# Three issue orders in a hybrid retention and sparse-attention block: angle tables behind the squares' sum, first indexer scores and the latent's sum of squares behind projection matmuls

## The chip, the cores and the metric

The kernel runs on one core of a Trainium2 chip. The metric is the device time of one execution in microseconds (us), as the median of three runs. A core has five engines, each with its own instruction queue that is worked off in order: TensorE (PE), VectorE (DVE), ScalarE (ACT), GpSimd (POOL) and SyncE (SP, which here only issues DMAs).

## The reference

One layer over 1024 tokens of width 1024, one batch, fp32:

```python
h = rms_norm(x, norm_mix)
proj = h @ w_in        # one projection, split into the inputs of both head groups
a = retention(rotary(r_q), rotary(r_k), r_v)            # 8 heads of 64, chunks of 64
c_kv = rms_norm(d_c, kv_norm)                           # latent of width 128
b = sparse_attention(q_nope, q_pe, c_kv, k_pe, i_q, i_k, i_w, w_uk, w_uv)
# per token: score = sum_h i_w[h] * relu(i_q[h] . i_k * 32**-0.5), the 256 best keys,
# then softmax attention over these keys alone
y = concat(norm(a) * silu(r_g), b * silu(d_g)) @ w_out + x
y = y + sigmoid(rms_norm(y, norm_ple) @ w_ple_gate) * (p @ w_ple_proj)
out = rms_norm(y, norm_final)
```

## The kernel before

Tokens are taken in 8 tiles of 128. Matrix products are made to fp32 accuracy by splitting both operands into a high and a low part and adding three products (hi·hi, hi·lo, lo·hi); ACT writes the high part of a weight (`whi`, L222) and POOL the low part (`wlo`, L223). The work is written as a program of tiles, and a scheduler with a modelled timeline sets the order of the instructions on each engine from the data dependences, the buffers and priorities; the engines then work their queues off in order.

**Input stage.** x is loaded transposed in 8 pieces. `load_x` makes xhi on ACT (L257) and xlo on DVE (L258). `add_squares` squares each piece on ACT (L265) and adds it to `acc` on DVE (L266). PE runs the first projection as pieces come (L300 to L302), then sums `acc` over the partitions (L365), and DVE and POOL make the reciprocal root `rstd` of it (`rsqrt`, L314 to L323; POOL's power at L319). The angle tables cos and sin for the indexer (cosx, sinx) and for retention (cosr, sinr) are made by `angles` and `tables` (L330 to L343): DVE reduces the angles (L331, L335, L336, three passes of L338, L339), ACT takes the sines and squares (L340 to L342). `spread` (L349 to L355) turns rstd into a row over all partitions, `rstd_b`, and the tables are multiplied by it (L369).

**Projections.** `n_chunk` (L461 to L492) makes token-major projections: per chunk of 256 columns and per token tile 24 matmuls of 128x256 (L472 to L474; called N below), evacuated by ACT (nst, L475), finished on POOL (L485) and stored by SP (L490) or ACT (L492); chunks come in the order 2, 3, 0, 1 and then 4, 5. The first N need a PSUM bank that ACT frees by copying the first projection out (L360, `it`). `t_block` (L304 to L312) makes column-major blocks of 48 matmuls of 128x512 (called T): blocks 0 to 7 are retention's, block 8 the latent, blocks 9 to 11 the attention's queries.

**Indexer.** The indexer's queries and keys are rotated (L378 to L384), split (`il`, POOL L238), stored to DRAM (L392 to L415) and loaded again as `ks` (L431) and per token tile as `qs` (L436, L437). Score matmuls (L449) run by token tile in the order TI = 7, 6, 4, 2, 3, 5; ACT takes the relu (`rel`, L450), DVE adds the heads up (`sc`, L452 and L454).

**Search and choice.** For each row of tokens the threshold of the 256th score is searched on keys made by DVE (`key`, L600, L601): three tiles on DVE (counts L624, thresholds L633 to L650) and three on ACT (counts L640, L643, L645). The choice steps on DVE (L677 to L689) then write the mask `bias` for each tile.

**Latent.** Block 8 gives the latent; `cq` is its square (ACT L523), `pk` its sum over partitions on PE (L526).

**Rest.** `prep_v` (L722 to L731, ACT L730 and DVE L731 make the values' high and low parts `vd`) and `prep_k` (L733 to L745) prepare the attention; `retention_load` (SP L789) and `retention_split` (ACT L803, DVE L804: `qz`) prepare retention. Then attention, retention, output projection, gate and last norm run.

Of the kernel before, what the change touches and what calls it, by code (L numbers as in the profile page):

```python
# [15 lines left out]
OP = mybir.AluOpType  # L16
# [6 lines left out]
NT = 8  # L23
# [25 lines left out]
TI = [7, 6, 4, 2, 3, 5]  # L49
# [104 lines left out]
def _body(ctx, nc, tc, ap, dbg):  # L154
    V, A, G, T, Y = nc.vector, nc.scalar, nc.gpsimd, nc.tensor, nc.sync

    def f(t):
        return t.bitcast(F32)

    def pool(name, **kw):  # L160
        return tc.tile_pool(name=name, bufs=kw.pop("bufs", 1), reuse_waits="tile", **kw)

# [18 lines left out]
    ones1 = cpool.tile([128, 1], F32, name="ones1")  # L181
# [31 lines left out]
    xhi = [xpool.tile([128, S], FR, name=f"xhi{k}") for k in range(NT)]  # L213
    xlo = [xpool.tile([128, S], FR, name=f"xlo{k}") for k in range(NT)]
# [28 lines left out]
    acc = p1p.tile([128, S], F32, name="acc")  # L243
# [16 lines left out]
    def add_squares(k):  # L260
        raw = raws[k // 2][:, k % 2]
        if k == 0:
            A.activation(acc, raw, AF.Square)
        else:
            A.activation(raw, raw, AF.Square)  # L265
            V.tensor_tensor(out=acc, in0=acc, in1=raw, op=OP.add)  # L266

    w1 = []
    zero = p1p.tile([128, 512], BF, name="zero")
# [6 lines left out]
    for k in range(NT):  # L276
# [6 lines left out]
            Y.dma_start(posi, rows_to_all(ap["pos"], S))  # L283
        if k > 0:
            add_squares(k - 1)
    add_squares(NT - 1)
    Y.dma_start(same, ap["cst"][:, CF:CN])
    Y.dma_start(retn_b, rows_to_all(ap["ret_norm"], 512))

# [14 lines left out]
    def t_block(b, outs):  # L304
        ws = [load_w(ap["w_t"][b, kg], 128) for kg in range(2)]
        for h in range(2):
            sl = slice(512 * h, 512 * h + 512)
            for k in range(NT):
                wh, wl = (t[:, k % 4] for t in ws[k // 4])
                T.matmul(outs[h], wh, xhi[k][:, sl], start=k == 0, stop=False)  # L310
                T.matmul(outs[h], wh, xlo[k][:, sl], start=False, stop=False)  # L311
                T.matmul(outs[h], wl, xhi[k][:, sl], start=False, stop=k == 7)  # L312

    def rsqrt(out, ssum, n, w):  # L314
        a = tiny.tile([128, 16], F32, name="rs_a")[:, :w]
# [11 lines left out]
    cosx = wk("cosx")  # L327
    sinx = wk("sinx")

    def angles(col, cos_t):  # L330
        V.tensor_scalar(cos_t, posi, cst[:, CV + col:CV + col + 1], None, op0=OP.mult)  # L331

    def tables(cos_t, sin_t):
        ang, kk = cos_t, sin_t
        V.tensor_scalar(kk, ang, 1.0 / (2.0 * math.pi), MAGIC, op0=OP.mult, op1=OP.add)  # L335
        V.tensor_scalar(kk, kk, -MAGIC, None, op0=OP.add)  # L336
        for c in CODY:
            V.scalar_tensor_tensor(ang, kk, -c, ang, op0=OP.mult, op1=OP.add)  # L338
        V.tensor_scalar(ang, ang, PI_LO, -PI_LO, op0=OP.min, op1=OP.max)  # L339
        A.activation(sin_t, ang, AF.Sin)  # L340
        A.activation(cos_t, ang, AF.Sin, scale=0.5)
        A.activation(cos_t, cos_t, AF.Square)  # L342
        V.tensor_scalar(cos_t, cos_t, -2.0, 1.0, op0=OP.mult, op1=OP.add)  # L343

    angles(1, cosx)
    tables(cosx, sinx)
    angles(0, cosr)

    def spread(dst, col):  # L349
        for h in range(2):  # L350
# [81 lines left out]
    for i in TI:  # L432
        w = 128 * (i + 1)
        qs = ixp.tile([96, 8, 128], FR, name="qs", bufs=2)
        tsl = slice(128 * i, 128 * i + 128)
        Y.dma_start(f(qs)[0:64], d_iq[:, :, :, tsl].rearrange("n r h t -> (n r) h t"))  # L436
        Y.dma_start(f(qs)[64:96], d_iq[0, :, :, tsl])  # L437
        so = OFF[i] - OFF[2]
        dst = sc[:, so:so + w]
        for h in range(8):  # L440
            rel = wk("rel")
            if h % 4 > 1 if w <= 512 else h % 3 > 1:
                pbs = [(c0, min(w, c0 + 512), nb("ib")) for c0 in range(0, w, 512)]
            else:
                pbs = [(0, w, big())]
            for b0, b1, pb in pbs:
                for c0 in range(b0, b1, 512):
                    c1 = min(b1, c0 + 512)
                    T.matmul(pb[:, c0 - b0:c1 - b0], qs[:, h], ks[:, c0:c1], start=True, stop=True)  # L449
                A.activation(rel[:, b0:b1], pb[:, :b1 - b0], AF.Relu, scale=32.0 ** -0.5)  # L450
            if h == 0:
                V.tensor_scalar(dst, rel[:, :w], wi[:, i, 0:1], 0.0, op0=OP.mult, op1=OP.add)  # L452
            else:
                V.scalar_tensor_tensor(dst, rel[:, :w], wi[:, i, h:h + 1], dst, op0=OP.mult, op1=OP.add)  # L454
        V.memset(sc[0:64, so + w - 64:so + w], -3.0e38)
# [5 lines left out]
    def n_chunk(c, func, place=nb):  # L461
        ws = [load_w(ap["w_n"][c, kg], 256) for kg in range(4)]
        for tg in range(2):
            for a in range(4):
# [5 lines left out]
                for k in range(NT):  # L470
                    wh, wl = (t[:, k % 2] for t in ws[k // 2])
                    T.matmul(pb[:, a % 2], xhi[k][:, tsl], wh, start=k == 0, stop=False)  # L472
                    T.matmul(pb[:, a % 2], xhi[k][:, tsl], wl, start=False, stop=False)  # L473
                    T.matmul(pb[:, a % 2], xlo[k][:, tsl], wh, start=False, stop=k == 7)  # L474
                A.activation(st[:, a % 2], pb[:, a % 2], func, scale=rstd[:, j:j + 1])  # L475
                if a % 2 == 0:
                    continue
# [45 lines left out]
    A.activation(cq, cr, AF.Square)  # L523
    pk = nb("ib")
    for j in range(NT):
        T.matmul(pk[:, j:j + 1], cq[:, 128 * j:128 * j + 128], ones1, start=True, stop=True)  # L526
    rkv = cpool.tile([128, NT], F32, name="rkv")
    rsqrt(rkv, pk[:, :NT], 128, NT)

# [699 lines left out]
```

## Time and profile before

| | |
|---|---|
| median of 3 runs | 828.8 us (828.28 to 830.05) |
| profiled execution | 826.33 us |
| its span in the profile | 824.5 us |
| mean granted TensorE clock | 0.969 |
| PE busy | 763.3 us, 93% |
| DVE busy | 596.7 us, 72% |
| ACT busy | 477.3 us, 58% |
| POOL busy | 313.6 us, 38% |

The span runs from the first to the last instruction in the profile; the execution's own time is 1.8 us longer. The busy shares are means over stages with different limits, so a stage has to be read by itself.

### The profile page before, as it was taken

Reading aid. Unit: us, or ns where it says so; the run is one execution under the profiler, and the core shown is the slowest. Engines: PE = TensorE matmul, PEld = TensorE weight load, DVE = VectorE, ACT = ScalarE, POOL = GpSimd, SP = SyncE. Lnnn points to the kernel's source line nnn. Section 1 sums busy time; section 2 is a strip of 40 time slices with the busy share of each in tenths; the row PEclk is TensorE's granted clock in tenths of the full one; section 3 lists DMA queues with packets and bytes.
Section 4 is the critical chain, followed back from the end, with each engine's and each line's share of the span. In section 5 each row is a group of like instructions: output and inputs, shape, how many; then the busy total and the mean of one; then the engine's idle time right before and its main releaser. Section 6 shows DMA issues by size and latency. Waiting matters only on the chain.

```text
span 824.5 us, 12686 instructions
## 1 busy us (share of the span) xinstructions
PE 763.3 (93%) x4415; PEld 661.8 (80%) x4415; DVE 596.7 (72%) x1270; ACT 477.3 (58%) x1041; POOL 313.6 (38%) x237
## 2 busy tenths in 40 slices
PE   8979699979999979999889887999999999899995
PEld 5768699968888868998788776788878887688885
DVE  5948178999999999998768777556565655653655
ACT  7543267729995699971667565543464454334333
POOL 3725625452775544730037667520261101310110
PEclk9979899989999999999999998999999999999999
DMA  8312924221533122532647755773554446542511
GB/s 316 99 40 93 235 76 115 65 78 31 179 101 112 52 103 85 177 113 77 166 116 197 204 157 172 237 249 133 158 190 172 161 172 206 202 153 78 178 52 52
DMA packets 68159, 114.42 MB, mean 139 GB/s; under 512 B 6048, under 2 KB 37664, under 8 KB 68096
## 3 DMA queue, kind: packets, MB, share of 16 engines
q1 hardware_dynamic: 64480, 107.06, 41.9%
q10 hardware_dynamic: 3616, 6.55, 2.2%
q8 instruction: 35, 0.57, 0.3%
q14 instruction: 28, 0.23, 0.1%
HBM read 75.97 MB, written 37.62 MB: 138 GB/s over the span
## 4 chain that ended last, share of the span: by engine, by line
PE 50%; DVE 31%; ACT 5%; DMA 5%; issue 4%; POOL 2%; SPq 1%; POOLq 0%; ACTq 0%; DVEq 0%
DVE res L624 8%; PE lg L1146 6%; PE rb L1146 5%; PE rb L1076 4%; PE rb L1077 3%; PE rb L1078 3%; PE tp L937 3%; PE nb L472 2%; PE nb L473 2%; PE nb L474 2%; DMA qk<-d_f 2%; PE lg L915 1%; PE oo L973 1%; PE lg L914 1%; PE oo L972 1%
## 5 line engine op out<-in xcount | busy, mean ns | idle before, releaser
L640 ACT ACTIVATE ajunk<-key,cthr 128x1024 bf16<-128x1024 int16 (+5 forms) x96 | 95.7, 997 | 27.5 <-DVE key L601 15.0
L223 POOL TENSOR_TENSOR wlo<-wraw,whi 128x512 fp32r<-128x512 f32 (+1 forms) x58 | 88.0, 1533 | 53.6 <-ACT whi L222 53.5
L473 PE MATMUL nb<-wlo,xhi 128*128 128x256 f32 x256 | 74.5, 292 | 5.5 <-POOL wlo L223 5.5
L472 PE MATMUL nb<-whi,xhi 128*128 128x256 f32 x256 | 75.0, 295 | 2.2 <-ACT nst L475 1.5
L624 DVE TENSOR_SCALAR_CACHE_REDUCE res<-key,athr 128x384 f32<-128x384 int16 (+5 forms) x96 | 75.5, 786 | 1.8
L474 PE MATMUL nb<-whi,xlo 128*128 128x256 f32 x256 | 74.3, 291 | 0.0
L319 POOL TENSOR_TENSOR rs_y<-rs_a,mhalf 128x1 f32<-128x1 f32 (+1 forms) x26 | 27.1, 1046 | 122.8 <-DVE rs_a L318 120.3
L944 DVE TENSOR_TENSOR t<-tp,t 128x512 fp32r<-128x512 f32 (+1 forms) x72 | 45.7, 643 | 30.3 <-ACT t L943 29.9
L920 ACT ACTIVATE lm<-lm,mxv 128x128 f32<-128x128 f32 (+3 forms) x64 | 49.3, 772 | 21.4 <-DVE mxv L919 20.9
L943 ACT ACTIVATE t<-tp 128x512 fp32r<-128x512 f32 (+1 forms) x72 | 39.0, 556 | 37.8 <-PE oo L973 27.2
L310 PE MATMUL big<-xhi,whi 128*128 128x512 f32 x144 | 56.1, 392 | 0.4 <-DVE mb L384 0.4
L311 PE MATMUL big<-xlo,whi 128*128 128x512 f32 x144 | 56.2, 391 | 0.0
L473 PEld LDWEIGHTS nb<-wlo,xhi 128*128 128x128 f32 x256 | 51.1, 200 | 6.3 <-POOL wlo L223 5.7
L312 PE MATMUL big<-xhi,wlo 128*128 128x512 f32 x144 | 55.8, 390 | 0.0
L472 PEld LDWEIGHTS nb<-whi,xhi 128*128 128x128 f32 x256 | 50.9, 200 | 4.3 <-ACT nst L475 2.7
L454 DVE SCALAR_TENSOR_TENSOR sc<-rel,wi,sc 128x1024 f32<-128x1024 f32 (+5 forms) x42 | 47.3, 1129 | 7.5 <-ACT rel L450 4.9
L474 PEld LDWEIGHTS nb<-whi,xlo 128*128 128x128 f32 x256 | 51.0, 199 | 0.7
L937 PE MATMUL tp<-cst,lm 128*128 128x128 f32 x288 | 47.8, 282 | 2.9 <-DVE t L944 2.1
L916 DVE CUSTOM_DVE_ANT_0 lm<-lg,bias 128x512 f32<-128x512 f32 (+2 forms) x64 | 36.7, 585 | 13.6 <-PE tp L937 6.4
L937 PEld LDWEIGHTS tp<-cst,lm 128*128 128x128 f32 x288 | 35.2, 145 | 9.0 <-DVE t L944 3.8
L222 ACT ACTIVATE whi<-wraw 128x512 fp32r<-128x512 f32 (+1 forms) x58 | 34.9, 611 | 12.3 <-PE nb L474 3.0
L972 PE MATMUL oo<-t,vd 128*128 128x256 f32 (+1 forms) x144 | 38.6, 287 | 3.1 <-ACT t L943 2.6
(497 smaller groups left out, 2451.6 us busy)
## 6 DMA issues: line engine op xcount, KB each, us to landing
wraw<-in_w_t SPq DMA_DIRECT2D x26, 256.0 KB, 2.8
wraw<-in_w_n SPq DMA_DIRECT2D x24, 256.0 KB, 2.7
d_f<-o SPq DMA_DIRECT2D x8, 512.0 KB, 3.1
qk<-d_f SPq DMA_DIRECT2D x16, 256.0 KB, 3.5
ql<-d_qs SPq DMA_DIRECT2D x16, 256.0 KB, 5.2
qh<-d_qs SPq DMA_DIRECT2D x32, 128.0 KB, 4.8
twr<-in_w_out SPq DMA_DIRECT2D x8, 512.0 KB, 5.6
xt<-in_x SPq DMA_DIRECT2D x8, 512.0 KB, 4.1
```

The lines of the kernel that those rows point to most:

```text
L223: G.tensor_tensor(out=lo, in0=raw, in1=f(hi), op=OP.subtract)
L310: T.matmul(outs[h], wh, xhi[k][:, sl], start=k == 0, stop=False)
L311: T.matmul(outs[h], wh, xlo[k][:, sl], start=False, stop=False)
L312: T.matmul(outs[h], wl, xhi[k][:, sl], start=False, stop=k == 7)
L472: T.matmul(pb[:, a % 2], xhi[k][:, tsl], wh, start=k == 0, stop=False)
L473: T.matmul(pb[:, a % 2], xhi[k][:, tsl], wl, start=False, stop=False)
L474: T.matmul(pb[:, a % 2], xlo[k][:, tsl], wh, start=False, stop=k == 7)
L624: V.tensor_scalar(junk, src[:, KS[i]], thr[:, n:n + 1], 0.0, op0=op, op1=OP.add, accum_out=cnt[:, n:n + 1])
L640: A.activation(junk[:, :128 * (i + 1)], src[:, KS[i]], AF.Sign, bias=self.thr[:, n:n + 1], accum_out=cnt[:, n:n + 1])
L920: A.activation(lm[:, :w], lm[:, :w], AF.Exp, bias=mx, scale=0.125, accum_out=den[:, a, h:h + 1])
L937: T.transpose(tp[:, o:o + 128], pt[a][:, ks_], ident)
L1146: T.matmul(po[c.start // 512][:, c.start % 512:c.start % 512 + c.stop - c.start], a, b[:, c], start=k == 0 and m == 0, stop=k == n - 1 and ...
```

## The change

Three orders of issue are added; no operation is added, taken away or resized.

1. `angles` and `tables` are traced inside a block that puts every instruction they issue on DVE behind the last add of squares, `squares`, which `add_squares` now returns.
2. The score matmuls of the first two tiles in TI (7 and 6) get an ordering edge behind the last matmul that `n_chunk` issues for chunk 3, tile 2.
3. The eight matmuls of `pk` get an ordering edge behind the last matmul of the first half of block 9, the first query block.

All three are edges between instructions of one engine, so none adds a semaphore. The scheduler lays everything else out anew around them.

```diff
+    marks = {}
+    def behind(ins, mark):
+        marks.setdefault(mark, []).append(ins)
+    def mark(name, ins):
+        for x in marks.pop(name, []):
+            tc.add_manual_dep(x.ins, ins.ins.name,
+                              mybir.DependencyInfo(mybir.DependencyClass.NoSync, mybir.DependencyReason.DATA),
+                              reason="order of issue")
...
-            V.tensor_tensor(out=acc, in0=acc, in1=raw, op=OP.add)
+            return V.tensor_tensor(out=acc, in0=acc, in1=raw, op=OP.add)
...
-    add_squares(NT - 1)
+    squares = add_squares(NT - 1)
...
-                T.matmul(outs[h], wl, xhi[k][:, sl], start=False, stop=k == 7)
+                last = T.matmul(outs[h], wl, xhi[k][:, sl], start=False, stop=k == 7)
+            if h == 0:
+                mark(f"block {b}", last)
...
-    angles(1, cosx)
-    tables(cosx, sinx)
-    angles(0, cosr)
+    with tc.issue_after(squares.ins):
+        angles(1, cosx)
+        tables(cosx, sinx)
+        angles(0, cosr)
...
-                    T.matmul(pb[:, c0 - b0:c1 - b0], qs[:, h], ks[:, c0:c1], start=True, stop=True)
+                    m = T.matmul(pb[:, c0 - b0:c1 - b0], qs[:, h], ks[:, c0:c1], start=True, stop=True)
+                    if i in TI[:2]:
+                        behind(m, "chunk 3 tile 2")
...
-                    T.matmul(pb[:, a % 2], xlo[k][:, tsl], wh, start=False, stop=k == 7)
+                    last = T.matmul(pb[:, a % 2], xlo[k][:, tsl], wh, start=False, stop=k == 7)
+                mark(f"chunk {c} tile {j}", last)
...
-        T.matmul(pk[:, j:j + 1], cq[:, 128 * j:128 * j + 128], ones1, start=True, stop=True)
+        behind(T.matmul(pk[:, j:j + 1], cq[:, 128 * j:128 * j + 128], ones1, start=True, stop=True), "block 9")
```

**DVE, input stage.** acc is the sum of squares, xlo the low parts of x, cosx, sinx, cosr, sinr the tables on their way. Before:

```order
L338 SCALAR_TENSOR_TENSOR cosx<-sinx,cosx 128x1024
L258 SCALAR_TENSOR_TENSOR xlo_120<-xraw,vecs,xhi_112 128x1024
L258 SCALAR_TENSOR_TENSOR xlo_121<-xraw,vecs,xhi_113 128x1024
L338 SCALAR_TENSOR_TENSOR cosr<-sinr,cosr 128x1024
L266 TENSOR_TENSOR acc<-acc,xraw 128x1024
L338 SCALAR_TENSOR_TENSOR cosx<-sinx,cosx 128x1024
L338 SCALAR_TENSOR_TENSOR cosr<-sinr,cosr 128x1024
L266 TENSOR_TENSOR acc<-acc,xraw 128x1024
L338 SCALAR_TENSOR_TENSOR cosx<-sinx,cosx 128x1024
L338 SCALAR_TENSOR_TENSOR cosr<-sinr,cosr 128x1024
L266 TENSOR_TENSOR acc<-acc,xraw 128x1024
L339 TENSOR_SCALAR cosx<-cosx 128x1024
```

and of the change, where line 258 is 270, 266 is 278, 331 is 345, 335 is 349 and 336 is 350:

```order
L278 TENSOR_TENSOR acc<-acc,xraw 128x1024
L270 SCALAR_TENSOR_TENSOR xlo_119<-xraw,vecs,xhi_111 128x1024
L278 TENSOR_TENSOR acc<-acc,xraw 128x1024 x2
L270 SCALAR_TENSOR_TENSOR xlo_120<-xraw,vecs,xhi_112 128x1024
L270 SCALAR_TENSOR_TENSOR xlo_121<-xraw,vecs,xhi_113 128x1024
L278 TENSOR_TENSOR acc<-acc,xraw 128x1024 x2
L345 TENSOR_SCALAR cosx<-posi,cst 128x1024
L345 TENSOR_SCALAR cosr<-posi,cst 128x1024
L349 TENSOR_SCALAR sinx<-cosx 128x1024
L349 TENSOR_SCALAR sinr<-cosr 128x1024
L350 TENSOR_SCALAR sinx<-sinx 128x1024
L350 TENSOR_SCALAR sinr<-sinr 128x1024
```

Before, seven passes of the tables stand between these low parts and sums, and others ahead of them; now all low parts and sums come first, and the fourteen table passes follow in one stretch, ahead of `rs_a` of `rsqrt`.

**PE, where the first score matmuls stand.** nb <- whi, wlo, xlo are N matmuls, big and ib <- ks, qs the scores. Before:

```order
L474 MATMUL nb<-whi,xlo_120 128x256
L472 MATMUL nb<-whi,xhi_113 128x256
L473 MATMUL nb<-wlo,xhi_113 128x256
L474 MATMUL nb<-whi,xlo_121 128x256
L472 MATMUL nb<-whi,xhi_110 128x256
L449 MATMUL big<-ks,qs 128x512 x4
L449 MATMUL ib<-ks,qs 128x512 x2
L473 MATMUL nb<-wlo,xhi_110 128x256
L474 MATMUL nb<-whi,xlo_118 128x256
```

and of the change, where lines 472 to 474 are 489 to 491 and 449 is 464:

```order
L491 MATMUL nb<-whi,xlo_120 128x256
L489 MATMUL nb<-whi,xhi_113 128x256
L490 MATMUL nb<-wlo,xhi_113 128x256
L491 MATMUL nb<-whi,xlo_121 128x256
L464 MATMUL big<-ks,qs 128x512 x4
L464 MATMUL ib<-ks,qs 128x512 x2
L489 MATMUL nb<-whi,xhi_106 128x256
L490 MATMUL nb<-wlo,xhi_106 128x256
L491 MATMUL nb<-whi,xlo_114 128x256
```

Before, 205 N stand between the sum over partitions and the first score, the last of them in the middle of a tile; now 240 N, ten whole tiles, stand there. The transposes of `spread` stand behind 38 N instead of 48. To the last score of tile 2 there are 347 N from the first score, 355 before. The `pk` matmuls move by three matmuls: behind 36 of the 48 of block 9 instead of 33.

**DVE, choice steps.** qz is retention's split, vd the values, the other lines are the choice of one tile. Before:

```order
L686 SCALAR_TENSOR_TENSOR res<-junk 128x768
L687 SCALAR_TENSOR_TENSOR junk<-res,aneed,junk 128x768
L804 TENSOR_TENSOR qz_4551<-qk,qz_4550 64x4x128 x2
L688 SCALAR_TENSOR_TENSOR junk<-sc,akfin,junk 128x768
L689 TENSOR_SCALAR bias<-junk 128x768
L804 TENSOR_TENSOR qz_4556<-qk,qz_4555 64x4x128 x2
...
L687 SCALAR_TENSOR_TENSOR junk<-res,cneed,junk 128x640
L688 SCALAR_TENSOR_TENSOR junk<-sc,ckfin,junk 128x640
L689 TENSOR_SCALAR bias<-junk 128x640
L731 TENSOR_TENSOR vd_4365<-lg,vd_4365 128x8x64
L731 TENSOR_TENSOR vd_4366<-rb,vd_4366 128x8x64
L731 TENSOR_TENSOR vd_4367<-lg,vd_4367 128x8x64
```

and of the change, where line 687 is 705, 688 is 706, 804 is 822 and 731 is 749:

```order
L705 SCALAR_TENSOR_TENSOR junk<-res,aneed,junk 128x384
L822 TENSOR_TENSOR qz_4551<-qk,qz_4550 64x4x128
L706 SCALAR_TENSOR_TENSOR junk<-sc,akfin,junk 128x384
L822 TENSOR_TENSOR qz_4551<-qk,qz_4550 64x4x128
L707 TENSOR_SCALAR bias<-junk 128x384
L703 TENSOR_SCALAR junk<-sc,akfin 128x512
...
L749 TENSOR_TENSOR vd_4365<-lg,vd_4365 128x8x64
L749 TENSOR_TENSOR vd_4366<-rb,vd_4366 128x8x64
L705 SCALAR_TENSOR_TENSOR junk<-res,cneed,junk 128x640
L749 TENSOR_TENSOR vd_4367<-lg,vd_4367 128x8x64
L749 TENSOR_TENSOR vd_4368<-rb,vd_4368 128x8x64
L706 SCALAR_TENSOR_TENSOR junk<-sc,ckfin,junk 128x640
```

Before, the first qz came in the choice of the third tile (768 wide); now they come one by one in that of the first (384 wide) and the second. Before, the eight vd came behind the last choice; now six stand inside it, and the last two behind it. On ACT, nine of the 96 counts of line 640 stand behind the first copy of qz (L803) instead of four, and all copies and stores of `nst` stand ahead of the first vd copy (L730), where one store (L492) stood ahead of the fourth. On POOL, one scaling of `nst` (L485) fewer stands ahead of `xs` (L403) and ahead of the second `il` (L238), and the products `cg` and `sg` (L503) have moved behind four `wlo` that stood behind them. On SP, the first stores of `nst` (L490) now come behind the loads of `ks` and `qs`.

## Rows read from the trace of the kernel before

**Rows 1.** The head of the profile page: the span, and per engine the busy time, its share of the span and the number of instructions.

```profile
span 824.5 us, 12686 instructions
...
PE 763.3 (93%) x4415; PEld 661.8 (80%) x4415; DVE 596.7 (72%) x1270; ACT 477.3 (58%) x1041; POOL 313.6 (38%) x237
```

**Rows 2.** Busy time by stretch. Columns: start:end in us, length, then busy us and (x instructions) of PE, PE's weight loads, DVE, ACT and POOL, then the granted TensorE clock as a share of full speed, the busy share of the DMA engines, and GB/s.

```profile
80.00:100.00 20.00, 13.30 (x106) 12.75 (x107) 2.90 (x4) 5.30 (x9) 14.98 (x14) 0.94 0.88 205
100.00:120.00 20.00, 20.00 (x131) 18.81 (x131) 12.84 (x12) 13.17 (x19) 3.48 (x2) 0.89 0.39 118
...
160.00:200.00 40.00, 33.03 (x224) 30.55 (x223) 39.25 (x85) 23.67 (x62) 17.90 (x10) 0.91 0.19 53
200.00:280.00 80.00, 79.65 (x362) 65.82 (x361) 77.56 (x160) 63.85 (x176) 51.90 (x32) 1.00 0.33 109
280.00:360.00 80.00, 74.99 (x416) 66.03 (x415) 77.78 (x193) 77.56 (x204) 42.99 (x28) 0.96 0.38 124
...
411.00:824.50 413.50, 384.99 (x2243) 328.99 (x2242) 252.05 (x668) 200.91 (x418) 126.13 (x112) 0.98 0.50 161
```

**Rows 3.** PE's waits from 0 to 387 us, the longest ones: what waited, for what, us in total, times, longest.

```profile
PE big L449 <- DMA qs<-d_iq: 6.5, 1, 6.5
...
PE ib L365 <- DVE acc L266: 5.3, 1, 5.3
PE ib L526 <- ACT cq L523: 4.5, 1, 4.5
```

**Rows 4.** PE in order of time, around the sum over partitions, the start of the token-major matmuls and the first score matmuls. Columns: start us, us, engine, line, operation, out<-in, shape, count, [idle before and its releaser]. A matmul's duration overlaps the next one's; its pace is the step between starts.

```profile
42.38 0.39 PE L302 MATMUL nb<-xhi,wlo 128*128 128x512 f32 x1
...
48.10 3.58 PE L365 MATMUL ib<-ones,acc 128*128 128x1 f32 x16 [5.33 <-DVE acc L266]
...
52.16 0.58 PE L472 MATMUL nb<-whi,xhi 128*128 128x256 f32 x1 [0.49 <-ACT it L360]
52.54 0.42 PE L473 MATMUL nb<-wlo,xhi 128*128 128x256 f32 x1
52.75 0.41 PE L474 MATMUL nb<-whi,xlo 128*128 128x256 f32 x1
...
62.05 0.28 PE L472 MATMUL nb<-whi,xhi 128*128 128x256 f32 x1
62.17 0.28 PE L473 MATMUL nb<-wlo,xhi 128*128 128x256 f32 x1
...
99.59 2.05 PE L449 MATMUL big<-ks,qs 96*128 96x512 f32 x4 [6.49 <-DMA qs<-d_iq]
```

**Rows 5.** DVE from 0 to 50 us: first the two groups of line 338 (three passes for each table; columns: count | busy us, mean ns | idle before), which are a view by line.

```profile
L338 DVE SCALAR_TENSOR_TENSOR cosx<-sinx,cosx 128x1024 f32<-128x1024 f32 x3 | 5.8, 1947 | 0.0
L338 DVE SCALAR_TENSOR_TENSOR cosr<-sinr,cosr 128x1024 f32<-128x1024 f32 x3 | 4.7, 1577 | 0.0
```

**Rows 6.** DVE in order of time: two passes of line 338, the last add of squares, the last table row.

```profile
35.61 1.21 DVE L338 SCALAR_TENSOR_TENSOR cosr<-sinr,cosr 128x1024 f32<-128x1024 f32 x1
37.88 2.32 DVE L338 SCALAR_TENSOR_TENSOR cosx<-sinx,cosx 128x1024 f32<-128x1024 f32 x1
...
46.83 1.21 DVE L266 TENSOR_TENSOR acc<-acc,xraw 128x1024 f32<-128x1024 f32 x1
...
48.56 0.68 DVE L339 TENSOR_SCALAR cosr<-cosr 128x1024 f32<-128x1024 f32 x1
```

**Rows 7.** ACT in order of time, where the tables are done and the first PSUM bank is freed.

```profile
48.68 1.06 ACT L340 ACTIVATE sinx<-cosx 128x1024 f32<-128x1024 f32 x1 [8.19 <-DVE cosx L339]
...
51.53 0.57 ACT L360 ACTIVATE it<-nb 128x512 f32<-128x512 f32 x1
```

**Rows 8.** POOL in order of time, ahead of the indexer's rotated projections.

```profile
77.10 2.29 POOL L485 TENSOR_TENSOR nst<-nst,retn_b 128x512 f32<-128x512 f32 x1
```

**Rows 9.** The chain of waits: the load of the first score tile's queries, from its issue (start us, us until it landed).

```profile
95.12 4.33 DMA qs<-d_iq
```

**Rows 10.** DVE in order of time: two score accumulations of the same shape.

```profile
162.48 3.17 DVE L454 SCALAR_TENSOR_TENSOR sc<-rel,wi,sc 128x768 f32<-128x768 f32 x1
...
166.82 1.01 DVE L454 SCALAR_TENSOR_TENSOR sc<-rel,wi,sc 128x768 f32<-128x768 f32 x1
```

**Rows 11.** POOL in order of time, beside the first of them.

```profile
158.93 3.08 POOL L503 TENSOR_TENSOR cg<-cosr,gam 128x1024 f32<-128x1024 f32 x1 [4.20 <-DVE junk L600]
```

**Rows 12.** DVE in order of time, the choice step of the first of three tiles.

```profile
345.01 1.47 DVE L687 SCALAR_TENSOR_TENSOR junk<-res,aneed,junk 128x384 bf16<-128x384 f32 x1
```

**Rows 13.** SP in order of time: the first load of retention's queries and keys.

```profile
348.09 0.86 SPq L789 DMA_DIRECT2D qk<-d_f  x2
```

**Rows 14.** ACT in order of time: the first retention split, two copies of 64 partitions.

```profile
351.35 1.29 ACT L803 ACTIVATE qz<-qk 64x512 fp32r<-64x512 f32 x2 [0.16 <-DMA qk<-d_f]
```

**Rows 15.** DVE in order of time, at the end of the choice steps.

```profile
386.91 0.33 DVE L689 TENSOR_SCALAR bias<-junk 128x640 bf16<-128x640 bf16 x1
...
393.02 0.69 DVE L731 TENSOR_TENSOR vd<-rb,vd 128x512 fp32r<-128x512 f32 x1 [3.12 <-ACT vd L730]
```

**Rows 16.** ACT's queue in order of time: the DMA issue ahead of the fourth value copy.

```profile
391.98 0.37 ACTq L492 DMA_DIRECT2D d_dg<-nst  x1
```

**Rows 17.** DVE's waits from 160 to 400 us, the longest.

```profile
DVE vd L731 <- ACT vd L730: 3.9, 2, 3.1
```

## The prediction

> **What bounds the kernel now.** I read the head of the page first: PE is busy for 763.3 of 824.5 us, DVE for 596.7 [rows 1]. Means hide stages, so the busy time by stretch comes next [rows 2]. It shows three of them. Up to about 100 us no engine is full: from 80 to 100 us PE works 13.30 of 20 us. From 160 to 360 us DVE is full (39.25 of 40, 77.56 of 80, 77.78 of 80): this is the search for the best keys. PE does its projections beside it and has time left in it (33.03 of 40, 74.99 of 80). From 411 us to the end PE is full (384.99 of 413.50) with attention, output and gate, an order that the change leaves nearly alone; I let this stretch move as a whole. So the change pays only by what brings the first scores, hence the search, and then the end of the choice steps forward.
>
> PE's waits up to 387 us [rows 3] name the places: 6.5 us for the load of qs ahead of the first score, 5.3 us for the squares' sum, 4.5 us for cq ahead of pk. The first is on the path to the search. The second is followed by another wait that keeps its place, below. The third lies where DVE is full.
>
> **Edge 1, the tables.** PE ends the first projection at 42.77 us and waits until the last add lets it sum at 48.10 [rows 4]. DVE ends that add at 48.04 and the tables at 49.24 [rows 6]: sums and tables share one engine that is full by then. The new order does the sums first and leaves the total as it is, so the sum over partitions starts when PE is ready, at some 42.8 us. But the first N needs a PSUM bank that ACT frees only at its `it`, and ACT stands at the sine until the tables are done: sine at 48.68 for 1.06 us, `it` at 51.53 for 0.57 us [rows 7], first N at 52.16 [rows 4]. In the new order `it` comes directly behind the first sine, not behind three passes. With the tables ready at the same time `it` ends at 48.68 + 1.06 + 0.57 = 50.3 us, and N starts **1.8 us** earlier instead of 5.3. The wait has only moved.
>
> The unknown is the tables' own pace in one stretch. The six passes of line 338 took 5.8 + 4.7 = 10.5 us [rows 5], each either 1.21 or 2.32 us [rows 6], so three of each. All at the short time would end the tables 3.3 us earlier, all at the long one 3.3 us later. I take no change, since POOL's work beside them is the same.
>
> **Edge 2, the first scores.** PE stood ready for them at 99.59 - 6.49 = 93.1 us. It now starts 1.8 us earlier and has 240 N instead of 205 in front, at a pace of 62.17 - 62.05 = 0.12 us: 35 x 0.12 = 4.2 us. PE comes to the scores at 93.1 - 1.8 + 4.2 = 95.5 us. The load was issued at 95.12 and landed 4.33 us later, at 99.45 [rows 9]. Ahead of it, one scaling of nst (2.29 us, [rows 8]) less stands on POOL, the rotation's rstd row comes behind 38 N instead of 48 (1.2 us), and all of it starts 1.8 us earlier: 99.45 - 5.3 = 94.2 us. So the load lands just ahead of PE, and the first score moves from 99.59 to 95.5: **-4.1 us**.
>
> The wait of 6.49 us had an aftermath. From 100 to 120 us the granted clock was 0.89 [rows 2], and (1 - 0.89) x 20 = 2.2 us of full speed were lost, at the lower of the two levels after PE had stood still. The same is seen after the wait at 48.10: N at steps of 52.75 - 52.54 = 0.21 us, later 0.12 [rows 4]. Without the wait this goes: **-2.2 us**. To the last score of the third tile eight N fewer stand in between, up to -1.0 us; I take 0, since DVE's accumulations pace the scores there too. The search then starts 6.3 us earlier, and being bound by DVE it ends 6.3 us earlier.
>
> **Choice steps and values.** After the last choice pass, at 386.91 + 0.33 = 387.24 us [rows 15], eight vd passes of 0.69 us follow, and DVE waits for ACT's copies between them for 3.9 us, 3.1 at once [rows 17], at the place where ACT's queue held a store, issued at 391.98 [rows 16]. Now six vd stand inside the choice and the store stands ahead of all copies. The waits go as far as PE has the values ready before: 0 to -3.9 us. I take **-3.4**, leaving half a microsecond for the last two.
>
> **Edge 3 and the rest.** The pk matmuls come three matmuls later; the wait of 4.5 us falls in part or whole, but PE has 5 us to spare from 280 to 360 us [rows 2] and DVE covers it: price 0. Were that cover gone, -4.5 us. What it does buy is lead: the projections, and with them the loads behind them, come earlier against the search. The new order uses that lead by placing qz early on DVE (a rival, below): price 0 in the sum, +5.5 at worst.
>
> **Sum:** -4.1 - 2.2 - 3.4 = -9.7 us. Against the profiled execution, 826.33, that is 816.6 (span 824.5 to 814.8); that execution lies 2.5 below the median of 828.8, so the forecast is 828.8 - 9.7 = **819.1 us**, with 815 to 823.5 for its own range (tables 3.3 us either way, values 0 to -3.9).
>
> **Rivals.** *Larger gain.* Tables faster by part of the 3.3 us (-2.0), the eight N (-1.0), and fewer collisions of DVE with POOL: one accumulation of 128x768 took 3.17 us and the next 1.01 [rows 10], with a cg product on POOL from 158.93 [rows 11]; with cg and sg behind four wlo, 3.17 - 1.01 = 2.2 us may go. 819.1 - 5.2 = 813.9, a range of 811 to 815.
>
> *Half of it eaten.* The qs load gains nothing. From 80 to 100 us the DMA engines were busy for 0.88 of the time [rows 2]; if it lands at 99.45 as before, the front gives nothing, and only the values' 3.4 us remain: 825.4, a range of 823.5 to 827. The Trainium skill (Trainium Kernel Development and Optimization, Key Constraints) says that DMAs of all issuing queues run on the same 16 DMA engines and interleave; by that rule an earlier issue helps less than the difference of the issue times, and the sum would tend to this 825.4. No row of before tells how far.
>
> *No change.* Search and end are set by something the edges don't reach, such as the loads of weights: 827.1 to 830.5, around 828.8.
>
> *Slower: DVE stands at qz.* DVE ended the first L687 at 345.01 + 1.47 = 346.48 us [rows 12]. Directly behind it now stands the first qz, which needs ACT's first half at 351.35 + 0.64 = 351.99 [rows 14], itself released by a load that SP issued at 348.09 [rows 13]. If projections and loads come no earlier than before, DVE stands there until 351.99, however early the search began: +5.5 us against before, the front gain lost. With the values' -3.4 that is +2.1, 830.9; without them (PE late for vd as well) +5.5, 834.3. A range of 830.5 to 834.3. It decides by how much earlier that load comes: below 0.4 us the kernel is slower, from 3.8 us on it is faster. For it: the order placed qz so early, and both engines work in order. Against it: PE starts the projections of this stretch 6.3 us ahead and loses up to 4.5 us of wait besides. The Trainium skill (TensorE: Matmul & The Clock Gate, Architectural detail) has ACT's and DVE's queues as strict first in, first out; by that rule a late qz holds up all choice passes behind it and the time would be this 830.9.
>
> **How the numbers follow.** Forecast 0.54, larger 0.14, eaten 0.12, no change 0.07, slower 0.13. About 0.2% (1.7 us) is what a measurement of this kernel can tell from no change. Faster: 0.54 + 0.14 + 0.12 = 0.80; within 0.2%: 0.07; slower: 0.13. The range goes from 811 (the larger gain whole) to 828.8 (half of no change), which leaves out the slower case and the rest of no change, 0.17.
>
> **What would show it.** The sum over partitions starts at about 43 us, and ACT's first `it` ends near 50.3. The first score starts near 95.5 us with a wait under 1 us, and the clock from 95 to 115 us is near 1.0. The search and choice end near 381 us, the wait of vd for ACT is under 1 us, and the first attention matmuls come some 10 us earlier, with the length of the stretch behind them unchanged. It is wrong if a qs wait of several microseconds remains ahead of the first score, if DVE's waits show qz for more than 2 us, or if the stretch from 411 us on changes its length by over 2 us.

## The result and the profile after

The kernel with the three orders takes 818.06 us in the median of four runs (816.92 to 820.07), beside 829.42 for the kernel before: a ratio of 0.9877, 95% interval 0.9839 to 0.9915. The profiled execution took 816.92 us with a span of 815.0. The forecast was 819.1 and a span of 814.8. The number was right; the sum behind it was not, and the profile shows where.

The head of the page after, to be read against [rows 1]:

```profile
span 815.0 us, 12678 instructions
...
PE 756.9 (93%) x4415; PEld 657.8 (81%) x4415; DVE 588.4 (72%) x1270; ACT 477.4 (59%) x1041; POOL 309.0 (38%) x237
```

DVE does the same 1270 instructions in 588.4 us instead of 596.7. No pass was taken away, so some passes have become shorter. The busy time by stretch, with the columns of [rows 2]:

```profile
80.00:100.00 20.00, 9.85 (x70) 9.45 (x69) 1.40 (x2) 1.81 (x4) 4.21 (x9) 0.77 0.81 191
100.00:120.00 20.00, 20.00 (x148) 19.22 (x147) 10.96 (x8) 12.37 (x19) 9.33 (x7) 0.98 0.43 108
...
160.00:200.00 40.00, 35.76 (x243) 33.39 (x242) 39.42 (x79) 22.45 (x55) 20.43 (x12) 0.91 0.23 63
200.00:280.00 80.00, 80.00 (x354) 66.24 (x353) 72.15 (x174) 69.78 (x192) 52.56 (x34) 1.00 0.36 116
280.00:360.00 80.00, 78.02 (x475) 69.52 (x474) 77.75 (x192) 77.31 (x206) 41.74 (x28) 1.00 0.36 122
...
401.00:815.00 414.00, 385.36 (x2237) 329.91 (x2235) 252.21 (x665) 200.43 (x417) 126.57 (x112) 0.97 0.50 162
```

From 80 to 100 us PE works even less than before (9.85 us, before 13.30), at a granted clock of 0.77 instead of 0.94; the last stretch is as it was. PE's longest waits up to 387 us and PE in order of time:

```profile
PE nb L489 <- ACT nst L493: 13.7, 3, 9.6
PE nb L489 <- ACT it L375: 8.7, 1, 8.7
PE lg L744 <- DVE vd L749: 2.7, 2, 2.4
```

```profile
49.96 0.58 PE L489 MATMUL nb<-whi,xhi 128*128 128x256 f32 x1 [8.70 <-ACT it L375]
...
97.32 0.58 PE L489 MATMUL nb<-whi,xhi 128*128 128x256 f32 x1 [9.58 <-ACT nst L493]
...
106.19 1.09 PE L464 MATMUL big<-ks,qs 96*128 96x512 f32 x4
```

The three waits of [rows 3] are gone, the one for `it` is 8.70 us long (0.49 in [rows 4]), and one of 9.58 us has come: the first score starts at 106.19 us, 6.6 us later than before, not 4.1 earlier. Gone too is a wait that [rows 3] leaves out, the second longest of the kernel before, at 171.8 us:

```profile
PE nb L473 <- POOL wlo L223: 5.5, 1, 5.5
```

What ended the wait of 9.58 us is in ACT's and SP's queues:

```profile
96.79 0.47 ACT L493 ACTIVATE nst<-nb,rstd 128x256 f32<-128x256 f32 x1 [10.80 <-DMA d_g<-nst]
```

```profile
87.78 1.02 SPq L446 DMA_DIRECT2D ks<-d_ik  x2
...
89.52 0.60 SPq L508 DMA_DIRECT2D d_g<-nst  x1
90.22 0.41 SPq L446 DMA_DIRECT2D ks<-d_ik  x1
90.67 1.25 SPq L451 DMA_DIRECT2D qs<-d_iq  x2
...
92.63 2.77 SPq L508 DMA_DIRECT2D d_g<-nst  x5
```

There are three nst buffers. ACT can't evacuate N into the next one before an earlier one is stored, and SP's stores now stand behind the loads of ks and qs. PE, with no PSUM bank free, stands still.

The gain is made later. DVE in order of time at the first choice stage (from the first key, akfin, to the second, ckfin) and at the end of the last one, and POOL beside it:

```profile
343.48 0.16 DVE L695 TENSOR_TENSOR akfin<-akth,av 128x3 int32<-128x3 int32 x1
...
347.68 0.62 DVE L705 SCALAR_TENSOR_TENSOR junk<-res,aneed,junk 128x384 bf16<-128x384 f32 x1
...
351.28 0.26 DVE L707 TENSOR_SCALAR bias<-junk 128x384 bf16<-128x384 bf16 x1
...
363.37 0.16 DVE L695 TENSOR_TENSOR ckfin<-ckth,cv 128x3 int32<-128x3 int32 x1
...
386.63 0.68 DVE L749 TENSOR_TENSOR vd<-rb,vd 128x512 fp32r<-128x512 f32 x1
```

```profile
338.52 3.64 POOL L797 MEMSET qz<- 128x1024 f32 x4
342.12 1.30 POOL L594 TENSOR_TENSOR uk1l<-wraw,uk1h 128x512 fp32r<-128x512 f32 x1
345.47 1.29 POOL L817 TENSOR_TENSOR kk<-qk,kk 128x512 fp32r<-128x512 f32 x1 [2.05 <-ACT kk L816]
```

The pass that took 1.47 us in [rows 12] takes 0.62, and L707 0.26. Before, as L689, it took 3.24 us beside the four qz memsets:

```profile
348.09 3.24 DVE L689 TENSOR_SCALAR bias<-junk 128x384 bf16<-128x384 bf16 x1
```

```profile
347.57 3.64 POOL L779 MEMSET qz<- 128x1024 f32 x4
```

The whole stage, before and after (columns of [rows 2]):

```profile
340.57:367.69 27.12, 26.63 (x222) 26.42 (x221) 26.43 (x28) 22.14 (x57) 16.91 (x12) 1.00 0.48 159
```

```profile
343.48:363.37 19.89, 19.41 (x160) 19.00 (x160) 19.31 (x28) 19.33 (x52) 5.54 (x4) 1.00 0.27 88
```

DVE does the same 28 passes in both and is full in both (26.43 of 27.12 us, 19.31 of 19.89), so the stage is shorter because these passes are. POOL works 5.54 us in it instead of 16.91. The memsets now come before the stage, and there they are not free: the small pass behind the last round of counts, which takes 0.16 us with POOL idle, stands beside them.

```profile
339.01 3.17 DVE L651 TENSOR_SCALAR ad<-acnt 128x3 bf16<-128x3 f32 x1
```

So the 3.0 us that the memsets took from the choice are paid in the search. The rest of the 7.2 us, most of it lost beside POOL's splits of weights, does not come back there: the search as a whole is 1.7 us shorter.

The stages, each from the starts and ends of rows such as those above (first score matmul; first new threshold on DVE; the two keys; end of the eighth vd pass; end of prep_k's last kk pass; span), in us:

| | before | after | moved by | the stage's part |
|---|---|---|---|---|
| first score | 99.6 | 106.2 | +6.6 | +6.6 |
| first threshold | 178.1 | 182.7 | +4.6 | -2.0 |
| first choice begins | 340.6 | 343.5 | +2.9 | -1.7 |
| second choice begins | 367.7 | 363.4 | -4.3 | -7.2 |
| values done | 396.2 | 387.3 | -8.9 | -4.6 |
| prep_k done | 412.2 | 401.5 | -10.7 | -1.8 |
| span | 824.5 | 815.0 | -9.5 | +1.2 |

### The profile page after: what moved, and what is told of

Its sections match the earlier page's. It is cut to its first block, busy times and chain, and to the rows that moved or that the text cites. A ratio compares the mean times of both kernels' runs of the same rounds, so it can differ in the third digit from the quotient of the medians.

```text
span 815.0 us, 12678 instructions
## 1 busy us (share of the span) xinstructions
PE 756.9 (93%) x4415; PEld 657.8 (81%) x4415; DVE 588.4 (72%) x1270; ACT 477.4 (59%) x1041; POOL 309.0 (38%) x237
## 4 chain that ended last, share of the span: by engine, by line
PE 56%; DVE 25%; DMA 8%; issue 3%; ACT 3%; SPq 3%; POOL 2%; POOLq 0%; DVEq 0%; ACTq 0%
PE lg L1164 6%; PE rb L1164 5%; DVE res L642 5%; PE rb L1094 3%; PE rb L1095 3%; PE rb L1096 3%; PE tp L955 3%; PE nb L489 3%; PE big L323 3%; PE big L322 3%; PE big L324 3%; PE nb L490 3%; PE nb L491 3%; DMA qk<-d_f 2%; DVE sc L471 2%
## 5 line engine op out<-in xcount | busy, mean ns | idle before, releaser
L658 ACT ACTIVATE ajunk<-key,cthr 128x1024 bf16<-128x1024 int16 (+5 forms) x96 | 95.5, 995 | 14.3 <-DVE key L619 10.5
L490 PE MATMUL nb<-wlo,xhi 128*128 128x256 f32 x256 | 74.8, 293 | 0.7 <-POOL wlo L235 0.7
L938 ACT ACTIVATE lm<-lm,mxv 128x128 f32<-128x128 f32 (+3 forms) x64 | 49.3, 772 | 20.1 <-DVE mxv L937 19.4
L471 DVE SCALAR_TENSOR_TENSOR sc<-rel,wi,sc 128x1024 f32<-128x1024 f32 (+5 forms) x42 | 51.0, 1213 | 4.3 <-ACT rel L467 1.6
L490 PEld LDWEIGHTS nb<-wlo,xhi 128*128 128x128 f32 x256 | 51.4, 201 | 1.9 <-POOL wlo L235 1.4
L1097 DVE TENSOR_TENSOR xt<-rb,xt 128x512 f32<-128x512 f32 x32 | 22.0, 689 | 27.6 <-PE rb L1096 24.3
```

What stands on the lines that cost most here:

```text
L658: A.activation(junk[:, :128 * (i + 1)], src[:, KS[i]], AF.Sign, bias=self.thr[:, n:n + 1], accum_out=cnt[:, n:n + 1])
```

## Experiments

Two theories stand against each other. A: DVE's search carries the moment of the first scores to the end. B: the gain is made at the choice steps and the values, whatever the first score does.

**Which edge does it.** The program without the third edge has, on all five engines, the very order of the full change, and the program with the third edge alone that of the kernel before. Neither needed a run: the third edge does nothing here. Two kernels remain, the first edge alone:

```diff
-                    if i in TI[:2]:
+                    if False:
...
-        behind(T.matmul(pk[:, j:j + 1], ...), "block 9")
+        T.matmul(pk[:, j:j + 1], ...)
```

> The change with the first edge alone (tables behind the sums). Its order puts 180 N ahead of the first score, and the eight vd behind the last choice but one pass. Theory A (the search carries the front to the end): N starts at about 50 us as with all three edges, but the scores come 60 N earlier in PE's order, so the first score falls at about 95 to 98 us, and the end is 3 to 6 us ahead of the kernel before, 823 to 826 us. Theory B (the gain is made at the choice steps and the values, where the order of vd and of POOL's work decides): without vd inside the choice no gain from there, 826 to 830 us, whatever the first score does. An N wait for a store of nst of several us should stand here too, since SP's order of stores and loads is that of the full change.

and the second alone (`with tc.issue_after(squares.ins):` taken away, the third as above):

> The change with the second edge alone (scores of the first two tiles behind chunk 3, tile 2). 240 N ahead of the first score, two of the eight vd ahead of the last choice's third pass, SP's first stores of nst ahead of the loads as before. Theory A: the sums and tables as before, PE comes to the scores at 93.1 + 4.2 = 97.3 us, the load lands at 99.4, so the first score is at about 99.5 us with a wait of 2 us; the front gains 0 to 2 us, and with nothing else the time is 827 to 829. Theory B: vd and choice give 4 to 8 us, 820 to 825 us.

Measured: 817.27 us, ratio 0.9871 (0.9818 to 0.9924), and 813.75 us, ratio 0.9843 (0.9790 to 0.9897). Within the intervals, each alone gives what all give together. PE's waits and the two keys of the first edge alone:

```profile
PE big L464 <- DMA qs<-d_iq: 7.6, 1, 7.6
PE ib L544 <- ACT cq L541: 4.5, 1, 4.5
PE nb L490 <- POOL wlo L235: 2.7, 1, 2.7
```

```profile
339.26 0.16 DVE L695 TENSOR_TENSOR akfin<-akth,av 128x3 int32<-128x3 int32 x1
...
366.07 0.16 DVE L695 TENSOR_TENSOR ckfin<-ckth,cv 128x3 int32<-128x3 int32 x1
```

and of the second alone:

```profile
PE nb L489 <- ACT nst L493: 3.7, 2, 3.5
PE big L464 <- DMA qs<-d_iq: 3.5, 1, 3.5
```

```profile
339.52 0.16 DVE L695 TENSOR_TENSOR akfin<-akth,av 128x3 int32<-128x3 int32 x1
...
359.31 0.16 DVE L695 TENSOR_TENSOR ckfin<-ckth,cv 128x3 int32<-128x3 int32 x1
```

With the first alone the first score comes at 96.37 us, 3.2 ahead of before, and the choice stage keeps its length: 366.07 - 339.26 = 26.8 us. Theory B expected 826 or more of it and was wrong there: in this order all eight vd still stand behind the last choice, and still DVE's wait for them is gone, with the values done at 390.7 us. So the vd did not need a place inside the choice. With the second alone the first score comes at 100.1, 0.5 later than before, and the choice stage is 19.8 us. Theory A expected 827 to 829 of it and was wrong there. So the short choice stage belongs to the second edge. That kernel also lost the waits for cq (4.5) and wlo (5.5 us in the kernel before) and has one for nst of 3.5 us. Its projections lead the search: their last matmul ends at 372.9 us, before at 387.0, while its choice begins only 1.1 us earlier than before. That this lead brings SP's loads, and POOL's memsets and splits behind them, out of the choice stage is read from the order of these rows; no run changes the lead alone.

**Whether the wait of 9.6 us is SP's queue, and whether the end follows the front.** The stores of chunks 2 and 3 from POOL's queue, in the full change:

```diff
-                        Y.dma_start(dst[:, j - 1:j + 1], ...)
+                        (Y if c < 2 else G).dma_start(dst[:, j - 1:j + 1], ...)
```

> The full change, with the stores of chunks 2 and 3 (nst to d_g) issued from POOL's queue instead of SP's, so that they don't stand behind the loads of ks and qs. If the wait of 9.6 us on N for a free nst buffer comes from SP's queue, it falls below 3 us and the first score comes at 97 to 100 us instead of 106. Theory A: the end follows by 6 to 9 us, 809 to 812 us. Theory B: the end does not follow or by less than 2 us, 816 to 819 us.

and a fourth nst buffer, paid with a wlo buffer (`nst` from 3 to 4, `wlo` from 6 to 5):

> The full change with four nst buffers instead of three and, to make room, five wlo buffers instead of six. SP's queue is as late as in the change, but PE can run one pair of tiles further: 48 N at 0.12 us or 5.8 us of the 9.6 us wait go, first score at about 100 us. Theory A: 812 to 814 us. Theory B: 816 to 820 us. A wlo buffer less may cost up to 2 us in either.

The first: 812.28 us, ratio 0.9822 (0.9772 to 0.9872), first score at 99.8. The second: 806.93 us, ratio 0.9751 (0.9704 to 0.9798), first score at 98.5. N's waits for nst from 53 us to the first score, in this order:

```profile
PE nb L489 <- ACT nst L493: 3.0, 3, 1.9
```

```profile
PE nb L489 <- ACT nst L493: 1.4, 1, 1.4
```

The cause of the wait is shown: with either remedy no single wait for nst there is over 1.9 us. The second gained more than either theory expected. The end follows the front only in part: with the stores moved prep_k is done at 397.4, 4.1 us earlier for 6.4 at the first score; with four buffers at 400.9, 0.6 earlier for 7.7. The rest of the second one's gain lies behind prep_k: its last stage takes 805.1 - 400.9 = 404.2 us instead of 413.5. These stage lengths are those of the one execution that was profiled: 820.39 us for the first edge alone, beside its median of 817.27, and 810.18 for the moved stores, beside 812.28. Two runs asked why the last stage is shorter:

> The full change with five wlo buffers and three nst buffers, the half of nst4w that was only meant to make room. If nst4w's 11 us against the change came from the fourth nst buffer, this one is at 817 to 820 us with the wait on a store of nst of 9 to 10 us. If it came from the order that another buffer count brings in the later stages (its last stage was 401 us long, 410 in the change), this one is at 809 to 812 us too.

> The second edge alone (scores), with four nst and five wlo buffers. Theory: the first edge cost the pair some 4 us (813.8 us without it, 818 with), by the wait on a store of nst, which the fourth buffer takes away as well; so without both the front is at 97 to 100 us for the first score, the choice stage at 20 us as with all kernels that have the second edge, and the time is 803 to 808 us. If the first edge helps once the wait is gone, it is slower than nst4w's 806.9 by 1 to 3 us.

Five wlo buffers alone (822 us, ratio 0.9924, 0.9891 to 0.9957, later than either expectation) have the last stage at 415.4 us. They also leave a wait for nst of 5.8 us and the first score at 104.6, so a part of the 9.58 us went with the order that they bring, and the rest with the fourth buffer. The second edge with four nst buffers (808.53 us, ratio 0.9750, 0.9683 to 0.9817) has the last stage at 404.8, in an execution of 803.9 us. This kernel and the change with four buffers are not told apart; both beat the change and are the fastest kernels here.

> The kernel before with four nst and five wlo buffers, without any of the three edges. Two kernels with four nst buffers had a last stage (behind prep_k) of 401 us instead of 410. If that comes from the buffers alone, this kernel has it too and gains some 8 us, 819 to 822 us, with a choice stage of 27 us and the values' wait as in the kernel before. If it needs the edges, the last stage is 409 us and the time 826 to 829.

> The full change with four nst and five wlo buffers and the stores of chunks 2 and 3 from POOL's queue. nst4w alone: 806.9 us with a first score at 98.5 us and small waits for nst left (1.4, 1.6 and 3.4 us); the stores alone: 812.3. If the front still sets the end, the waits that are left go and it is 803 to 806 us. If it no longer does, 806 to 809 us.

The kernel before with four nst buffers took 827.4 us, ratio 0.9996 (0.9961 to 1.0031), with a last stage of 414.8 us; the change with four buffers and moved stores 813.81, ratio 0.9832 (0.9783 to 0.9881), with 415.1, slower than either expectation. So the short last stage comes with some orders that have four buffers and not with others. About half of the difference is idle time of PE: in the last stage PE stands for 14.6 us (the change with four buffers) and 16.0 (the second edge with four), and for 20.1 to 22.5 in the other kernels without added passes. Why these orders lose the waits is open. The kernel before with four buffers says more on the front. PE at its first score, and DVE at its two keys:

```profile
94.19 1.16 PE L449 MATMUL big<-ks,qs 96*128 96x512 f32 x4 [2.02 <-DMA qs<-d_iq]
```

```profile
336.82 0.16 DVE L677 TENSOR_TENSOR akfin<-akth,av 128x3 int32<-128x3 int32 x1
...
364.53 0.16 DVE L677 TENSOR_TENSOR ckfin<-ckth,cv 128x3 int32<-128x3 int32 x1
```

Its first score is 5.4 us ahead of before, and its time is not told apart from that of before. The lead is down to 3.8 us at the first choice (340.6 - 336.8), 2.6 at the values' end (396.2 - 393.6), 3.4 at the end of prep_k (412.2 - 408.8) and 0.9 in the span (824.5 - 823.6). The search from first threshold to first choice took 166.4 us, before 162.4, for the same work.

**Whether POOL's work beside the choice costs DVE time.** First, small memsets of a spare tile, added to the full change in the choice stage or beside the counts of the search:

```diff
             need = ...
+            if not self.scalar:
+                G.tensor_tensor(out=scr[:, :3], in0=need, in1=need, op=OP.add)
+                for _ in range(32):
+                    G.memset(scr, 0.0)
```

> The full change with 32 small memsets of a spare tile (128x128 bf16, 0.2 us each, 6.5 us in all) added on POOL, released when the first choice step starts. Theory A (DVE passes with POOL beside them wait for it, and the change gains by taking POOL's work out of the first choice stage): that stage, 19.9 us from the first key of the choice to the second, 27.1 us in the kernel before, grows by 4 to 6.5 us to 24 to 26 us, and the end of prep_k by as much. Theory B (POOL's work beside the choice costs nothing, the stage was shortened by something else): it stays at 20 us, give or take 0.5.

> The full change with 72 of the same memsets (14.6 us in all) added on POOL, nine released at the start of each of eight rounds of counting in the second half of the search. Theory A: the counts run beside POOL at their own time, and only the small passes between the rounds wait, at most 1 us a round where a memset still runs: DVE loses 0 to 4 us of its 161 us from the first threshold to the choice, less than the 32 memsets in the choice stage cost per us of POOL. Theory B (POOL slows whatever DVE does): 10 to 15 us lost.

Neither theory: the choice stage grew by 1.4 us to 21.3 (819.93 us, ratio 0.9889, 0.9854 to 0.9923), the search by 1.8 to 162.6 (820.99 us, ratio 0.9922, 0.9881 to 0.9963). In the kernel with the 32 memsets, where nothing is added to the search, the search took 159.1 us, so the 72 beside the counts may have cost up to 3.4 us. Per us of POOL such memsets hold DVE little at either place. So another kind of pass, one that reads two inputs, as POOL's own splits do (`G.tensor_tensor(out=scr, in0=scr, in1=scr, op=OP.add)`, 12 of them, or two in each of eight rounds):

> The full change with 12 added passes on POOL of another kind than in pool_choice: sums of a spare tile with itself (128x256 fp32, two inputs, estimated 0.7 us each from the 1.3 us of a pass of twice the width, 8 us in all), released when the first choice step starts. Small memsets there cost DVE 1.4 us for 14 us of POOL. If it depends on the kind of POOL's pass (one that reads holds DVE, a small memset hardly), the stage grows from 19.9 us to 24 to 28 us. If POOL's work beside the choice does not matter, it stays within 1.5 us of 19.9 again, and the shorter stage of the change has another cause.

> The same passes, two in each of eight rounds of counting in the second half of the search (16, 11 us in all). If counts run beside POOL at their own time and the choice passes do not, DVE loses at most 3 us of its 161 us in the search, against 4 to 8 us in pool_choice2 with fewer passes. If any DVE pass waits, it loses 7 to 11 us.

POOL's added passes by line, beside the choice and beside the counts (columns: count | busy us, mean ns | idle before), and the two keys of the first of these kernels:

```profile
L704 POOL TENSOR_TENSOR scr<-scr 128x256 f32<-128x256 f32 x12 | 11.8, 987 | 0.8
```

```profile
L721 POOL TENSOR_TENSOR scr<-scr 128x256 f32<-128x256 f32 x16 | 9.8, 612 | 1.0
```

```profile
343.14 0.16 DVE L697 TENSOR_TENSOR akfin<-akth,av 128x3 int32<-128x3 int32 x1
...
368.38 0.16 DVE L697 TENSOR_TENSOR ckfin<-ckth,cv 128x3 int32<-128x3 int32 x1
```

Twelve passes in the choice stage took 987 ns each and lengthened it from 19.9 to 25.2 us (824.6 us, ratio 0.9964, 0.9924 to 1.0003: nearly all of the gain undone, though a wait of PE of 5.1 us for a wlo behind them is part of it). Sixteen beside the counts took 612 ns each, and the search took 159.1 us, not longer than the change's 160.8, and 0.9 longer than the 158.2 of the kernel with the twelve, whose search has nothing added (818.33 us, ratio 0.9890, 0.9814 to 0.9965). So passes of this kind cost under 1 us beside the counts, and 5.3 beside the choice: that is shown. That the splits which left the choice stage gave back their time in the same way is read from the rows above; no run moves them alone.

## Why the prediction was right, and where it was not

**Tables (right in size).** `it` was to end at 50.3 us and N to start 1.8 earlier; N started at 49.96, 2.2 earlier, with 8.70 us of wait for `it`: the wait of the squares' sum only moved, as forecast. The tables' pace was less sure than it looks: all six passes of line 338 (now L352) took 1.21 us, for which the prediction would have had the tables 3.3 us earlier, and they ended at 48.93, 0.3 earlier.

**First score, -4.1 us (wrong: +6.6).** The failed step is the pricing of what stands ahead of the first score as 35 N at 0.12 us, and of SP's queue by what comes earlier in it alone. The stores that were moved behind the loads got no price. They free the nst buffers, and PE stands for 9.58 us behind them. With the stores on another queue the score came at 99.8, still 4.3 us later than forecast. The load itself came nearly as worked out: it was issued at 90.67 us, 4.45 earlier than before [rows 9], where 5.3 had been counted. With the first edge alone, where PE did wait for it, it was there at 96.37.

**Clock, -2.2 us (moved).** From 100 to 120 us the granted clock rose from 0.89 to 0.98, but from 80 to 100 it fell from 0.94 to 0.77. From first score to first threshold 2.0 us are gained; the standstill and the low clock behind it are now paid ahead of the score.

**The search carries the front to the end (wrong).** Choice began 2.9 us later, not 6.3 earlier, and the end still came 9.5 earlier. The kernel before with four nst buffers is the opposite case: 5.4 us earlier at the front, and at the end a ratio of 0.9996, which leaves room for 3.2 us at most (0.9961).

**Choice stage, 0 us with up to +5.5 (wrong: -7.2).** This is the term that was put at nothing. The lead of the projections was named, and spent on qz alone. It also moves POOL's memsets and splits out of the choice stage and beside the counts. The larger-gain rival had the mechanism, DVE beside POOL, at another place and with 2.2 us. DVE did not stand at qz: the slower rival is out.

**Values, -3.4 us (right in size, for another reason).** DVE's wait of 3.9 us is gone, and the stretch from the second choice to the last vd went from 28.5 to 23.9 us. But the first edge alone lost the wait too, with the vd behind the choice and one store still ahead of ACT's fourth copy, as before; there the store was issued at 384.19 us instead of 391.98 [rows 16]:

```profile
384.19 0.37 ACTq L510 DMA_DIRECT2D d_dg<-nst  x1
```

So it was the late store, and not the place of the vd. What made it late before stands in ACT's next row:

```profile
392.40 0.60 ACT L730 ACTIVATE vd<-rb 128x512 fp32r<-128x512 f32 x1 [3.43 <-DMA ql<-d_qs]
```

ACT's queue stood until a load of ql had landed, which SP had issued at 387.56 us; with the first edge alone the store waits for no such load. That prep_k gains 1.8 us more was not in the sum.

**Edge 3, 0 us (right, and for a simpler reason).** The third edge changes no engine's order. The wait for cq is gone with the second edge, and the lead that the prediction ascribes to the third is the second's too.

**Signs and range.** Of its signs that it is right, the first score near 95.5 us, the clock near 1.0 ahead of it and the end of the choice near 381 (386.1 measured) did not come, and of its signs that it is wrong none did: none named a wait for nst. The range of the forecast itself, to 823.5, is too narrow for its two terms, which give 819.1 + 3.3 + 3.4 = 825.8.

So the number held by luck: a term of the wrong sign at the front (10.7 us off, and 2.2 that only moved) met one that was missing at the choice (7.2) and smaller ones.

## What to carry to other kernels

Before an in-order DMA queue is reordered for a load, look at what buffers its stores set free, and how many tiles can be written until the first of them must be back. A front that comes earlier is worth something at the end only as far as the engine that is full in between does not lose it again; ask there which passes suffer from a neighbour, and place the neighbour's work beside those that don't, with its end ahead of the next one that does. An edge has to be judged by the order that comes out of it: one of these three did nothing, and the other two did not add up.

## What the runs showed of the hardware

The counts on DVE (one tile read, with an accumulated sum) run beside POOL at their own time: over the kernel before, the change, the two single edges, the moved stores and the change with four buffers, the counts of 384 elements that lay wholly inside POOL's busy time took 0.604 us on the mean (74 of them), and so did the others (118); of 768 elements 1.012 and 1.011 us (77 and 115). The small pass behind each round of counts does wait: in the same traces it took 0.61 us more than its 0.16 on the mean where a POOL pass overlaps it (100), 3.0 at most, and 0.01 more where none does (92).

Both engines lose where they collide: POOL's added sums took 987 ns each beside the choice passes and 612 beside the counts.

A DVE pass can be held by several POOL passes in a row. The four qz memsets follow each other without a gap, and the pass that met the first of them ended behind the last, both before (L689 at 351.33 us, the memsets at 351.21) and in the change (L651 at 342.18 and 342.16). Among the small memsets, which lie 0.06 us apart, the same kind of pass was not held:

```profile
353.64 6.47 POOL L703 MEMSET scr<- 128x128 bf16 x23
```

```profile
357.70 0.29 DVE L712 TENSOR_SCALAR bias<-junk 128x512 bf16<-128x512 bf16 x1
```

The Trainium skill (SBUF — State Buffer, SBUF: two separate sides) says that DVE and GpSimd share a port pair which whichever of them starts first holds for its whole instruction; for DVE it names passes in a fast two-port mode, and passes with two SBUF inputs against GpSimd passes that read SBUF. The traces agree for the last group and for the counts: the choice pass of [rows 12], with two inputs, took 1.47 us beside POOL's splits and 0.62 without, and the counts, which are in neither group, lost nothing.
